# Elementwise work beside two chunked recurrences: POOL to VectorE, a norm by heads on ScalarE, and a later fetch

## The chip, the cores and the metric

The kernel runs on one core of a Trainium2 chip. Five engines work beside each other, each through its own instruction queue in order: PE (TensorE matmul; PEld is its weight load), DVE (VectorE), ACT (ScalarE), POOL (GpSimd) and SP (SyncE, which here only issues DMAs). The metric is the device time of one execution in microseconds (us).

## The reference, cut to what matters

Two residual layers over 2048 tokens of width 1024 and a final norm. Layer 0 mixes by retention (4 heads) and stick-breaking attention (4 heads); layer 1 is an RWKV-7 recurrence with 16 heads of 64. After each layer an embedding `p[i]` is projected, gated and added.

```python
def block(args):                                   # stick-breaking, per block of 128 queries
    z = jnp.einsum('bqhd,bkhd->bhqk', q_blk, k) * scale
    log_1mb = jnp.where(mask, log_sigmoid(-z), 0.0)
    after = lax.cumsum(log_1mb, axis=3, reverse=True) - log_1mb
    w = jnp.where(mask, jnp.exp(log_sigmoid(z) + after), 0.0)
    return jnp.einsum('bhqk,bkhd->bqhd', w, v)

def step(state, inp):                              # RWKV-7, per token
    sk = jnp.einsum('bhvk,bhk->bhv', state, kk_t)
    state = state*w_t - sk*(kk_t*a_t) + v_t*k_t
    return state, jnp.einsum('bhvk,bhk->bhv', state, r_t)

y = head_norm(y, LNX_EPS) * lnx_g + lnx_b          # mean and variance over the 64 of a head
y = y + sum(r*k*r_k) * v                           # "bonus"
h = h + (y*silu(g)) @ w_out
h = h + sigmoid(h @ ple_gate) * (p @ ple_proj)
```

## The kernel before, in words

All large products are split into three fp32r products (high and low parts of both factors, `mm3`, L258 to L260), each 128 by 128 by 512; below they are called dense products. The sequence is done in two halves of 1024 tokens. The stages in order of time: layer 0's mixers of the first half, its tail (`tail`) and layer 1's projections (`l1_proj`); layer 0's mixers of the second half (to about 1900 us, the stick-breaking attention last); then the first half's recurrence merged with layer 0's tail of the second half; `l1_proj` of the second half; the second half's recurrence merged with layer 1's tail of the first half and of the first 512 tokens of the second; and a last tail block of 512 tokens.

The attention (L682 to L721) scores two blocks of 128 queries against up to 512 keys: PE computes z, ACT two sigmoids, DVE a reversed running product `rr` (the scan, L712), POOL copies the carry (L711) and multiplies `be` by `rr` (L721), PE transposes `be`, ACT and DVE split the result (L218, L219) and PE multiplies by the values.

A recurrence (`recur`) has 16 chunks of 64 tokens. Each chunk has small 64-wide products: `gram` (L1490, for the chunk three ahead; none for the last three), `inv` (a triangular inverse, one chunk ahead), and the state chain `chunk`: x (L1615), u (L1593), s (L1630), y. The next state is formed at L1638 and L1639 on two halves of the partitions, `par` 0 on DVE and `par` 1 on POOL. `post` norms the y of the chunk before: mean on DVE, subtraction on POOL (L1670), square on ACT (L1671), variance on DVE, scaling, `lnx` gain and bonus on POOL (L1675, L1677, L1678).

The merged tails (`tail_lean`) work on blocks of 512 tokens: eight output columns of the out projection, then eight of the gate projection (24 dense products each), the latter with 6 of the embedding's (`pp`). `gated` fetches the next block's inputs (L943 and on: DMA `stage` and `g`, two multiplications on DVE, a sigmoid), one column ahead of each gate column. The third block of the last merged stage reads what the recurrence beside it has just written, and is `may` only when its first eight chunks are done (`self.ready`).

`merge` hands out the two streams' instructions by fixed costs (`COST`, `RATIO`), the recurrence with a lead in priority. A scheduler then orders every engine's queue by a modelled timeline; so an operation that changes engine also moves others.

Of the kernel before, what the change touches and what calls it, by code (L numbers as in the profile page):

```python
# [9 lines left out]
F32 = mybir.dt.float32  # L10
# [3 lines left out]
AF = mybir.ActivationFunctionType  # L14
ALU = mybir.AluOpType
# [6 lines left out]
NB = D // P  # L22
# [8 lines left out]
C = 64  # L31
# [102 lines left out]
class Trunk:  # L134
# [520 lines left out]
    def attention(self, w, es):  # L655

        nc, tc, dd = self.nc, self.tc, self.dd
# [9 lines left out]
        def attn(h):  # L667
# [3 lines left out]
            for g in (0, 1) if w == 0 else (2, 1, 0, 3):  # L671
# [3 lines left out]
                vt = sb.tile([P, 2, 4, P], F32R, tag="vg", name=self.u("vg"), bufs=4)  # L675
# [6 lines left out]
            def unit(qp, g, st):  # L682
                i0 = w * NTT + qp * 2
                carry = st["carry"]
                kt, vt = kv[g]
# [7 lines left out]
                for qi in range(2):  # L693
# [14 lines left out]
                    if carry[qi] is None:  # L708
                        nc.gpsimd.memset(rr[:, kw : kw + 1], 1.0)
                    else:  # L710
                        nc.gpsimd.tensor_copy(rr[:, kw : kw + 1], carry[qi])  # L711
                    nc.vector.tensor_tensor_scan(  # L712
# [7 lines left out]
                    carry[qi] = rr[:, 0:1]  # L720
                    nc.gpsimd.tensor_tensor(be, be, rr[:, 1 : kw + 1], op=ALU.mult)  # L721
                    c = be
# [195 lines left out]
    def tail_lean(self, es, parts):  # L918


        nc, i = self.nc, self.i
# [42 lines left out]
        def block(blk, staged, following):  # L964
# [39 lines left out]
            for ob in range(NB):  # L1004
# [10 lines left out]
                nwt = self.w_cols(i["ple_gate"][l], (ob + 1) * P, f"gate{l}") if ob + 1 < NB else None  # L1015
                if following:
                    while not following[0][-1]():
                        yield 1.0
                    ahead.append(gated(following, ob))
                yield from proj(wt, hs)  # L1020
# [8 lines left out]
                o = T("o", 2)  # L1029
                nc.gpsimd.tensor_tensor(o, hs[ob][0].bitcast(F32), hs[ob][1].bitcast(F32), op=ALU.add)  # L1030
                nc.vector.tensor_tensor(o, o, g, op=ALU.add)
                yield 1.3
                if ob == 0:
                    nc.scalar.activation(self.ssacc[:, sl], o, AF.Square)
                else:
                    nc.scalar.activation(g, o, AF.Square)
                    nc.gpsimd.tensor_tensor(self.ssacc[:, sl], self.ssacc[:, sl], g, op=ALU.add)
                if l == 1:
                    nc.vector.tensor_scalar_mul(o, o, self.col(V_GF, ob))
                nc.sync.dma_start(h1[:, ob, sl], o)  # L1040
                yield
            return ahead

# [384 lines left out]
    def recur(self, w, es, lean=False, early=0):  # L1428
# [178 lines left out]
        def chunk(s):  # L1607
# [27 lines left out]
            for par in range(2):  # L1635
                hs = half(par)
                nx = tmp[hs] if last else st[s + 1]["w"][hs, 0, par]
                nc.vector.tensor_tensor(tmp[hs], ps[hs], sv[hs, par], op=ALU.add)  # L1638
                (nc.gpsimd if par else nc.vector).tensor_tensor(  # L1639
                    nx, tmp[hs], self.pc[hs, :, s].unsqueeze(2).to_broadcast([64, NB, C]), op=ALU.mult  # L1640
                )
# [20 lines left out]
        def post(s):  # L1662
# [5 lines left out]
            nc.vector.tensor_reduce(mean, y, axis=mybir.AxisListType.X, op=ALU.add)  # L1668
            nc.vector.tensor_scalar_mul(mean, mean, 1.0 / C)
            nc.gpsimd.tensor_tensor(y, y, bc(mean), op=ALU.subtract)  # L1670
            nc.scalar.activation(sq, y, AF.Square)  # L1671
            yield
            nc.vector.tensor_reduce(var, sq, axis=mybir.AxisListType.X, op=ALU.add)
            rs = self.rsqrt(fin, var, 1.0 / C, LNX_EPS, NB, "yr")
            nc.gpsimd.tensor_tensor(y, y, bc(rs), op=ALU.mult)  # L1675
            yield
            nc.gpsimd.tensor_tensor(vt, vt, bc(bonus[:, s]), op=ALU.mult)  # L1677
            nc.gpsimd.tensor_tensor(y, y, lnx[0][0], op=ALU.mult)  # L1678
            nc.vector.tensor_tensor(vt, vt, lnx[1][0], op=ALU.add)
            yield  # L1680
# [210 lines left out]
```

## Time and profile before

| | us |
|---|---|
| median of 3 runs | 3787.74 (3785.84 to 3797.48) |
| the profiled execution | 3787.24 |
| its span, first to last instruction | 3785.5 |
| PE busy in the span | 3536.1 (93%) |
| DVE busy | 1954.3 (52%) |
| ACT busy | 1412.1 (37%) |
| POOL busy | 986.2 (26%) |

Busy shares are unions over the whole span. PE's small products overlap, so the sum over its groups is more than its busy time. The granted TensorE clock is a share of full speed: 1.00 is 2.4 GHz, 0.50 is 1.2 GHz, and what lies between is a mix of the two within a stretch.

### The profile page before, as it was taken

How to read it: one execution, taken by the hardware profiler on the slowest of the kernel's cores; microseconds unless marked ns; L12 is line 12 of the kernel's file. 1: busy time of each engine (PE TensorE's matmuls, PEld its weight loads, DVE VectorE, ACT ScalarE, POOL GpSimd, SP SyncE). 2: the span in 40 equal slices, each digit the busy share in tenths (PEclk: the TensorE clock that was granted, in tenths of full speed). 3: DMA queues.
4: the chain of work that ended last, by engine and by line, in shares of the span. 5: the costliest groups of instructions: out<-in, count | busy, mean ns of one | idle time of the engine just before them, and what ended most of it. 6: DMA issues, size and time to landing. Idle time of an engine off the chain costs nothing.

```text
span 3785.5 us, 66193 instructions
## 1 busy us (share of the span) xinstructions
PE 3536.1 (93%) x25929; PEld 2801.1 (74%) x25929; DVE 1954.3 (52%) x3884; ACT 1412.1 (37%) x2767; POOL 986.2 (26%) x1036
## 2 busy tenths in 40 slices
PE   8999999899999999998979999899988799999978
PEld 6888877777666788887767777677656677777757
DVE  4334541453675433457956756542574477567532
ACT  5233453344553221445522322243553233223233
POOL 4345543400000222455512312200000143122322
PEclk9999999999999999999969999599989799989989
DMA  6348866655587225546456665343575876556485
GB/s 234 103 170 268 226 191 208 208 168 177 194 260 272 74 95 171 174 107 134 88 150 203 177 179 150 110 143 123 185 240 179 203 226 200 156 166 197 161 284 179
DMA packets 593792, 675.14 MB, mean 178 GB/s; under 512 B 215764, under 2 KB 443976, under 8 KB 562504
## 3 DMA queue, kind: packets, MB, share of 16 engines
q1 hardware_dynamic: 510056, 577.95, 49.3%
q10 hardware_dynamic: 42848, 59.39, 4.4%
q0 software_dynamic: 40576, 33.56, 4.2%
q8 instruction: 205, 3.36, 0.4%
q14 instruction: 107, 0.88, 0.1%
HBM read 414.78 MB, written 255.98 MB: 177 GB/s over the span
## 4 chain that ended last, share of the span: by engine, by line
PE 32%; DMA 8%; DVE 7%; SPq 3%; ACT 1%; issue 1%; POOL 1%; ACTq 0%; POOLq 0%; DVEq 0%
PE pj L258 6%; PE pj L259 6%; PE pj L260 6%; PE g L1490 2%; PE y L1652 2%; PE s L1630 1%; PE y L1649 1%; DMA wraw<-in_odd_w_out 1%; DMA w<-parts 1%; PE u L1593 1%; DMA g<-g 1%; DVE prd L1521 1%; PE x L1615 1%; PE kt L1603 1%; DVE wb L1527 1%
## 5 line engine op out<-in xcount | busy, mean ns | idle before, releaser
L258 PE MATMUL pj<-act,w 128*128 128x512 f32 x1216 | 498.5, 414 | 20.3 <-ACT act L218 9.8
L260 PE MATMUL pj<-act,w 128*128 128x512 f32 x1216 | 498.2, 410 | 4.0 <-POOL w L219 4.0
L259 PE MATMUL pj<-act,w 128*128 128x512 f32 x1216 | 496.6, 409 | 0.4 <-POOL act L219 0.4
L258 PE MATMUL pj<-xs,w 128*128 128x512 f32 x768 | 298.4, 403 | 18.1 <-DMA w<-parts 6.5
L259 PE MATMUL pj<-xs,w 128*128 128x512 f32 x768 | 307.0, 400 | 5.2 <-DVE xs L219 5.1
L260 PE MATMUL pj<-xs,w 128*128 128x512 f32 x768 | 302.4, 397 | 0.0
L258 PEld LDWEIGHTS pj<-act,w 128*128 128x128 f32 x1216 | 237.8, 196 | 72.0 <-ACT act L218 11.3
L260 PEld LDWEIGHTS pj<-act,w 128*128 128x128 f32 x1216 | 237.7, 195 | 56.4 <-POOL w L219 4.9
L259 PEld LDWEIGHTS pj<-act,w 128*128 128x128 f32 x1216 | 238.5, 196 | 50.5 <-POOL act L219 0.8
L258 PE MATMUL pj<-w,act 128*128 128x512 f32 x640 | 259.0, 408 | 10.8 <-ACT sg L535 7.1
L712 DVE TENSOR_TENSOR_SCAN rr<-om,rr,ones 128x512 f32<-128x512 f32 (+3 forms) x160 | 216.7, 1361 | 77.1 <-ACT om L706 68.6
L259 PE MATMUL pj<-w,act 128*128 128x512 f32 x640 | 254.9, 398 | 0.0
L260 PE MATMUL pj<-w,act 128*128 128x512 f32 x640 | 253.5, 399 | 0.0
L721 POOL TENSOR_TENSOR be<-be,rr 128x512 f32<-128x512 f32 (+3 forms) x160 | 167.3, 1048 | 192.6 <-DVE rr L712 87.2
L219 POOL TENSOR_TENSOR w<-wraw,w 128x1024 fp32r<-128x1024 f32 x72 | 159.4, 2218 | 173.4 <-ACT w L218 152.1
L258 PEld LDWEIGHTS pj<-xs,w 128*128 128x128 f32 x768 | 146.9, 192 | 67.2 <-issue 15.6
L1490 PE MATMUL g<-xr,kb 64*128 64x128 f32 x1024 | 149.7, 309 | 34.9 <-DVE grb L1498 20.6
L259 PEld LDWEIGHTS pj<-xs,w 128*128 128x128 f32 x768 | 146.9, 191 | 43.5 <-DVE xs L219 11.8
L260 PEld LDWEIGHTS pj<-xs,w 128*128 128x128 f32 x768 | 147.0, 192 | 34.3 <-issue 3.3
L1490 PEld LDWEIGHTS g<-xr,kb 64*128 64x128 f32 x1024 | 121.6, 203 | 60.0 <-DVE grb L1498 22.2
L258 PEld LDWEIGHTS pj<-w,act 128*128 128x128 f32 x640 | 121.9, 191 | 39.2 <-ACT sg L535 10.3
L218 ACT CAST w<-wraw 128x1024 fp32r<-128x1024 f32 x105 | 104.4, 1000 | 123.0 <-PE pj L260 27.2
(364 smaller groups left out, 7760.2 us busy)
## 6 DMA issues: line engine op xcount, KB each, us to landing
w<-parts SPq DMA_DIRECT2D x145, 1024.0 KB
parts<-w SPq DMA_DIRECT2D x97, 1024.0 KB
wraw<-in_odd_w_in SPq DMA_DIRECT2D x32, 512.0 KB
ar<-ar SPq DMA_DIRECT2D x32, 512.0 KB
w<-v SPq DMA_DIRECT2D x128, 128.0 KB
xr<-ar SPq DMA_DIRECT2D x64, 256.0 KB
kb<-kb SPq DMA_DIRECT2D x32, 512.0 KB
kg<-dk POOLq DMA_DIRECT2D x24, 512.0 KB, 5.0
```

The source lines that it names most:

```text
L218: nc.scalar.copy(hi, src)
L219: (lo_eng or nc.vector).tensor_tensor(lo, src, hi.bitcast(F32), op=ALU.subtract)
L258: nc.tensor.matmul(ps, a[0], b[0], start=first, stop=False)
L259: nc.tensor.matmul(ps, a[0], b[1], start=False, stop=False)
L260: nc.tensor.matmul(ps, a[1], b[0], start=False, stop=last)
L712: nc.vector.tensor_tensor_scan(rr[:, 0:kw][:, ::-1], om[:, ::-1], self.ones.to_broadcast([P, kw]), rr[:, kw : kw + 1], op0=ALU.mult, op1=A ...
L721: nc.gpsimd.tensor_tensor(be, be, rr[:, 1 : kw + 1], op=ALU.mult)
L1490: nc.tensor.matmul(ps[:, j], kb[br, 4 * g + j], xr[br, par, 4 * g + j], start=True, stop=True)
L1521: nc.vector.tensor_tensor(pr[:, :k, :n], nb[:, m, k:].unsqueeze(1).to_broadcast([P, k, n]), wb[:, :k, m:k].to_broadcast([P, k, n]), op=ALU ...
L1527: nc.vector.tensor_tensor(wb[:, :k, k:], wb[:, :k, k:], pr[:, :k, :n], op=ALU.add)
L1593: nc.tensor.matmul(ps[hs, ob], lhs[hs, ob], rhs[hs, ob], start=True, stop=True)
L1652: nc.tensor.matmul(o, d["grb"][hs, ob], uv[hs, par, ob], start=False, stop=True)
```

## The change

On the engines: the attention's carry copy and product, the recurrence's second half of the next state, the bonus and gain products of the norm, and the tail's two additions go from POOL to VectorE. The norm of a chunk is done by heads on ScalarE: eight squares with the mean as bias and a sum taken along (which replace subtraction, square and variance), and eight scalings. The carried-out `gated` of a following block is taken up at a column only if the block may be read; if not, all that is missing is fetched at the end. What stays on POOL beside the recurrences is the split of weights that are read for the first time (L219) and DMAs.

```diff
@@ attention
-                        nc.gpsimd.tensor_copy(rr[:, kw : kw + 1], carry[qi])
+                        nc.vector.tensor_copy(rr[:, kw : kw + 1], carry[qi])
...
-                    nc.gpsimd.tensor_tensor(be, be, rr[:, 1 : kw + 1], op=ALU.mult)
+                    nc.vector.tensor_tensor(be, be, rr[:, 1 : kw + 1], op=ALU.mult)
@@ tail_lean
-                if following:
-                    while not following[0][-1]():
-                        yield 1.0
-                    ahead.append(gated(following, ob))
+                if following and following[0][-1]():
+                    ahead.append(gated(following, len(ahead)))
...
-                nc.gpsimd.tensor_tensor(o, hs[ob][0].bitcast(F32), hs[ob][1].bitcast(F32), op=ALU.add)
+                nc.vector.tensor_tensor(o, hs[ob][0].bitcast(F32), hs[ob][1].bitcast(F32), op=ALU.add)
...
-                    nc.gpsimd.tensor_tensor(self.ssacc[:, sl], self.ssacc[:, sl], g, op=ALU.add)
+                    nc.vector.tensor_tensor(self.ssacc[:, sl], self.ssacc[:, sl], g, op=ALU.add)
...
+            while following and len(ahead) < NB:
+                while not following[0][-1]():
+                    yield 1.0
+                ahead.append(gated(following, len(ahead)))
@@ recur, chunk
-                (nc.gpsimd if par else nc.vector).tensor_tensor(
+                nc.vector.tensor_tensor(
@@ recur, post
-            nc.vector.tensor_scalar_mul(mean, mean, 1.0 / C)
-            nc.gpsimd.tensor_tensor(y, y, bc(mean), op=ALU.subtract)
-            nc.scalar.activation(sq, y, AF.Square)
-            yield
-            nc.vector.tensor_reduce(var, sq, axis=mybir.AxisListType.X, op=ALU.add)
+            nc.vector.tensor_scalar_mul(mean, mean, -1.0 / C)
+            for o in range(NB):
+                nc.scalar.activation(
+                    sq[:, o], y[:, o], AF.Square, bias=mean[:, o : o + 1], accum_out=var[:, o : o + 1]
+                )
+            nc.vector.tensor_tensor(vt, vt, bc(bonus[:, s]), op=ALU.mult)
+            yield
             rs = self.rsqrt(fin, var, 1.0 / C, LNX_EPS, NB, "yr")
-            nc.gpsimd.tensor_tensor(y, y, bc(rs), op=ALU.mult)
-            yield
-            nc.gpsimd.tensor_tensor(vt, vt, bc(bonus[:, s]), op=ALU.mult)
-            nc.gpsimd.tensor_tensor(y, y, lnx[0][0], op=ALU.mult)
+            nc.vector.tensor_tensor(mean, mean, rs, op=ALU.mult)
+            for o in range(NB):
+                nc.scalar.activation(
+                    y[:, o], y[:, o], AF.Identity, scale=rs[:, o : o + 1], bias=mean[:, o : o + 1]
+                )
             nc.vector.tensor_tensor(vt, vt, lnx[1][0], op=ALU.add)
+            yield
+            nc.vector.tensor_tensor(y, y, lnx[0][0], op=ALU.mult)
```

Three places in the order. First VectorE near the end of the second half's attention (`rr` the scan, `wT` the split weights, `xr` and `grb` the recurrence's gram, `tds` its inverse, `wb` and `prd` the inner inverse). Before:

```order
L712 SCALAR_TENSOR_TENSOR rr_16094<-om_16093,rr_16094,ones 128x384
L1494 TENSOR_TENSOR xr_17604<-g_17842,k 64x512
L1576 COPY f_3410_17449<-f_3409_17432 32x256
L1498 TENSOR_TENSOR grb_17840<-g_17842,k 64x256
L219 TENSOR_TENSOR wT_16058<-tp_16066,wT_16057 128x4x128
L712 SCALAR_TENSOR_TENSOR rr_16107<-om_16106,rr_16107,ones 128x512
L219 TENSOR_TENSOR wT_16114<-tp_16115,wT_16113 128x4x128
L712 SCALAR_TENSOR_TENSOR rr_16150<-om_16149,rr_16150,ones 128x512
```

The same place now:

```order
L721 TENSOR_TENSOR be_16160<-be_16160,rr_16162 128x512
L712 SCALAR_TENSOR_TENSOR rr_16201<-om_16200,rr_16201,ones 128x512
L711 COPY rr_16213<-rr_16162 128x1
L1523 TENSOR_TENSOR prd_17455<-nb_17417,wb_17418 128x3x13
L219 TENSOR_TENSOR wT_16169<-tp_16170,wT_16168 128x3x128
L1544 STREAM_TRANSPOSE t_3337_16917<-tds_16371 128x512
L721 TENSOR_TENSOR be_16199<-be_16199,rr_16201 128x512
L712 SCALAR_TENSOR_TENSOR rr_16213<-om_16212,rr_16213,ones 128x512
```

Each scan now has its product and copy in the same queue, and the recurrence stands further back: from the first gram to the last scan there are four pairs of `xr` and `grb` and 23 rows of `prd` and `wb` fewer than before, and the first chunk's u and s products follow the attention's last, where before 35 z products came behind its first s products.

Second, PE where the tail's dense products end beside the first recurrence (`pp` the embedding's, `t` and `f` the inverse, `ssp` the sums of squares, which are the tail's last). Before, at the fourteenth chunk's u:

```order
L258 MATMUL pp_20696<-pT_18543,pw_20611 128x512
L259 MATMUL pp_20696<-pT_18544,pw_20611 128x512
L260 MATMUL pp_20696<-pT_18543,pw_20611 128x512
L1583 MATMUL t_4022_22416<-tds_16371,f_4018_22384 32x32 x16
L1081 MATMUL ssp_23337<-ones,ssacc 128x1 x4
L1593 MATMUL u_22545<-xs_22522,tds_16371 64x64
L1686 MATMUL yt_22482<-k,y_21993 128x128 x4
```

Now the same end stands at the twelfth chunk's u:

```order
L259 MATMUL pp_20787<-pT_18570,pw_20702 128x512
L1585 MATMUL t_3946_21874<-tds_16372,f_3942_21844 32x32 x16
L260 MATMUL pp_20787<-pT_18569,pw_20702 128x512
L1492 MATMUL g_22208<-xr_21963,kb_21966 128x128 x4
L1595 MATMUL u_22008<-xs_21985,tds_16372 64x64
L1492 MATMUL g_22253<-xr_21963,kb_21966 128x128 x4
L1083 MATMUL ssp_23545<-ones,ssacc 128x1 x4
```

From the second chunk to there the tail's 864 dense products stand in ten chunks, where they stood in twelve; four chunks follow that have none, where two did.

Third, SP's queue where the last merged stage fetches the third block (`stage` from the recurrence's output `yT`, `g` its gate). Before:

```order
L946 DMA stage_32424<-yT_26660 128x512
L946 DMA stage_32597<-yT_26660 128x512
L1464 DMA kb_31774<-kb_23272 128x8x128
L949 DMA g_31709<-g_23277 128x512
L1040 DMA h_4714_26658<-o_31651 128x512
```

Now:

```order
L946 DMA stage_32056<-yT_26868 128x512
L1466 DMA kb_32548<-kb_23480 128x8x128
L946 DMA stage_32063<-yT_26868 128x512
L949 DMA g_32030<-g_23485 128x512
L949 DMA g_32037<-g_23486 128x512
```

The gates' fetches followed one by one between the second block's stores; now the second block is over first. On PE the interval from the ninth to the tenth chunk of this recurrence has no dense product (18 before), that from the fifteenth to the sixteenth has 2 (78 before), and none is left behind the sixteenth (24 before).

## Rows read from the trace of the kernel before

**Rows 1.** The page's first part: busy time, share and instructions of each engine.

```profile
PE 3536.1 (93%) x25929; PEld 2801.1 (74%) x25929; DVE 1954.3 (52%) x3884; ACT 1412.1 (37%) x2767; POOL 986.2 (26%) x1036
```

**Rows 2.** Busy time in stretches: stretch, length, engines with counts, PEclk, DMA share, GB/s.

```profile
1740.00:1900.00 160.00, 143.59 (x1374) 121.05 (x1373) 143.74 (x222) 93.33 (x205) 87.83 (x124) 0.96 0.43 91
1900.00:1990.00 90.00, 70.35 (x878) 55.71 (x878) 47.79 (x116) 21.01 (x43) 13.25 (x11) 0.70 0.59 168
1990.00:2380.00 390.00, 381.80 (x4820) 299.63 (x4819) 246.76 (x578) 115.44 (x237) 99.36 (x80) 0.97 0.62 179
2380.00:2400.00 20.00, 20.00 (x237) 16.38 (x237) 11.59 (x47) 4.16 (x8) 6.80 (x6) 0.53 0.27 83
3020.00:3500.00 480.00, 461.20 (x5674) 358.67 (x5674) 318.39 (x734) 154.42 (x306) 139.71 (x104) 0.93 0.66 190
```

**Rows 3.** Groups by line, attention's end, 1720 to 1905; the last from 1740.

```profile
L712 DVE TENSOR_TENSOR_SCAN rr<-om,rr,ones 128x512 f32<-128x512 f32 (+3 forms) x57 | 74.2, 1302 | 0.9 <-ACT om L706 0.3
L219 DVE TENSOR_TENSOR wT<-tp,wT 128x512 fp32r<-128x512 f32 (+3 forms) x61 | 38.1, 630 | 14.3 <-ACT wT L218 13.4
L1494 DVE TENSOR_TENSOR xr<-g,k 64x512 f32<-64x512 f32 x20 | 13.7, 683 | 12.0 <-PE g L1490 11.8
L1521 DVE TENSOR_TENSOR prd<-nb,wb 128x39 f32<-128x39 f32 (+7 forms) x26 | 9.5, 364 | 0.4
...
L711 POOL COPY rr<-rr 128x1 f32<-128x1 f32 x40 | 16.1, 401 | 10.4 <-DVE prd L1521 5.1 <-DVE rr L712 5.1
...
L712 DVE TENSOR_TENSOR_SCAN rr<-om,rr,ones 128x512 f32<-128x512 f32 x44 | 62.5, 1421 | 0.8 <-ACT om L706 0.3
```

**Rows 4.** Groups by line, whole span: VectorE with and without POOL beside it.

```profile
L1370 DVE TENSOR_TENSOR_SCAN L<-scan,sg 128x512 f32<-128x512 f32 x32 | 39.2, 1224 | 88.0 <-ACT sg L1363 88.0
L219 DVE TENSOR_TENSOR act<-stage,act 128x512 fp32r<-128x512 f32 x80 | 66.1, 846 | 13.1 <-ACT act L218 9.6 <-PE pj L259 1.5 <-PE pj L260 1.3
L219 DVE TENSOR_TENSOR xs<-mxa,xs 128x512 fp32r<-128x512 f32 x128 | 88.6, 702 | 96.0 <-ACT xs L218 95.1
L1639 DVE TENSOR_TENSOR w<-xs,pc 64x512 f32<-64x512 f32 x30 | 30.4, 1015 | 0.3
```

**Rows 5.** Instructions of single lines: count, ns minimum/median/maximum, first and last start, form.

```profile
L1669 DVE TENSOR_SCALAR mean<-mean x32: 153/172/1256, 1908.4 to 3622.0; 128x8 f32<-128x8 f32 x32
L384 ACT ACTIVATION_READ_ACCUMULATOR sq<-x x8: 186/186/187, 5.9 to 19.4; 128x1 f32 x8
L1563 ACT COPY tds<-t x64: 238/257/259, 1834.7 to 3583.7; 16x128 f32<-16x128 f32 x64
L1671 ACT ACTIVATE t<-y x30: 617/622/635, 1909.9 to 3604.8; 128x512 f32<-128x512 f32 x30
```

**Rows 6.** PE in order of time: u of chunks 2, 4, 14, 15, 16; the tail's first dense product.

```profile
1911.01 1.97 PE L1593 MATMUL u<-xs,tds 64*64 64x64 f32 x32 [1.34 <-ACT xs L1617]
...
1932.21 0.79 PE L258 MATMUL pj<-act,w 128*128 128x512 f32 x1
...
2003.75 1.15 PE L1593 MATMUL u<-xs,tds 64*64 64x64 f32 x32
...
2376.30 0.33 PE L1593 MATMUL u<-xs,tds 64*64 64x64 f32 x2
...
2411.19 0.47 PE L1593 MATMUL u<-xs,tds 64*64 64x64 f32 x2 [0.46 <-ACT tds L1586]
...
2439.66 0.47 PE L1593 MATMUL u<-xs,tds 64*64 64x64 f32 x2 [0.46 <-ACT tds L1586]
```

**Rows 7.** VectorE in order of time: the attention's last scan.

```profile
1895.42 1.27 DVE L712 TENSOR_TENSOR_SCAN rr<-om,rr,ones 128x512 f32<-128x512 f32 x1
```

**Rows 8.** PE in order of time: two dense products that follow each other.

```profile
2469.81 0.39 PE L260 MATMUL pj<-xs,w 128*128 128x512 f32 x1
2470.04 0.39 PE L259 MATMUL pj<-xs,w 128*128 128x512 f32 x1
```

More of the change, by code (lines that the diff above doesn't have):

```diff
@@ L1668, in post @@
             nc.vector.tensor_reduce(mean, y, axis=mybir.AxisListType.X, op=ALU.add)
-            nc.vector.tensor_scalar_mul(mean, mean, 1.0 / C)
-            nc.gpsimd.tensor_tensor(y, y, bc(mean), op=ALU.subtract)
-            nc.scalar.activation(sq, y, AF.Square)
+            nc.vector.tensor_scalar_mul(mean, mean, -1.0 / C)
[4 more added lines that the diff above has]
+            nc.vector.tensor_tensor(vt, vt, bc(bonus[:, s]), op=ALU.mult)
             yield
-            nc.vector.tensor_reduce(var, sq, axis=mybir.AxisListType.X, op=ALU.add)
             rs = self.rsqrt(fin, var, 1.0 / C, LNX_EPS, NB, "yr")
-            nc.gpsimd.tensor_tensor(y, y, bc(rs), op=ALU.mult)
+            nc.vector.tensor_tensor(mean, mean, rs, op=ALU.mult)
[3 more added lines that the diff above has]
+                )
+            nc.vector.tensor_tensor(vt, vt, lnx[1][0], op=ALU.add)
             yield
-            nc.gpsimd.tensor_tensor(vt, vt, bc(bonus[:, s]), op=ALU.mult)
-            nc.gpsimd.tensor_tensor(y, y, lnx[0][0], op=ALU.mult)
-            nc.vector.tensor_tensor(vt, vt, lnx[1][0], op=ALU.add)
+            nc.vector.tensor_tensor(y, y, lnx[0][0], op=ALU.mult)
             yield
```

## The prediction, made before the kernel ran

> **What bounds the kernel now.** I read the busy line first: PE works 93% of the span, no other engine more than 52% [rows 1]. The reader is to see that work taken from POOL or given to VectorE counts only where PE waits for it. So I went to the stretches that the change touches, by windows [rows 2]. Beside the first recurrence, 1990 to 2380, PE is busy 381.80 of 390.00 us at a clock of 0.97; beside the second, 3020 to 3500, 461.20 of 480.00 at 0.93: PE is the bound in both, with VectorE at 63% and 66% and ScalarE near 30%. Two stretches differ. At the attention's end, 1740 to 1900, VectorE (143.74 of 160) is as full as PE (143.59). From 2380 to 2400, where the tail's dense products have run out, PE counts as busy for all 20.00 us, but at a clock of 0.53, near the lower level of 1.2 GHz: it works through one recurrence's chain of small products. Next I read groups by line at the attention's end [rows 3] and over the whole span [rows 4], single lines for prices [rows 5], and PE in order of time, for when each chunk's u product comes [rows 6]. What the change does to PE's order stands in the orders shown above; these u times price it.
>
> **Unit prices.** A dense product takes 0.23 us, from one start to the next [rows 8]. From the u of chunk 4 to that of chunk 14 are 372.55 us [rows 6]; 721 of the tail's dense products stand there in PE's order, 165.8 us, so an ordinary chunk costs (372.55 − 165.8) / 10 = 20.7 us without them. Chunks 2 to 4 take 92.74 us with the other 143 of the 864 (32.9), thus 29.9 each: a start loss of 9.2 a chunk, 18.4 in all. The two chunks without dense products take 34.88 and 28.47 [rows 6], mean 31.7, which is 11.0 above an ordinary chunk's own cost. That a dense-free chunk costs 11.0 more is the number on which most hangs.
>
> **Attention's end.** VectorE gets a product beside each of 57 scans and 40 copies. The nearest row for the product is L219's wT at 0.630 [rows 3], 35.9 us; for the copy a small VectorE operation of 0.172 [rows 5], 6.8 us (between nothing and POOL's own 16.1 [rows 3]). It is relieved in two ways. The scans took 1.421 us with POOL at work, the same operation in L1370 1.224 without [rows 3, 4]: 44 × 0.197 = 8.7. And four pairs of gram operations at 0.683 and 23 inner products at 0.364 [rows 3] now stand behind the last scan: 13.9. Left are 42.7 − 8.7 − 13.9 = 20.1 us more, against 16.3 us of VectorE idle [rows 2]. If all of that idle time can be used, the last scan comes 3.8 later, if none, 20.1. VectorE is the full engine and gets more than it gives away, so a gain is excluded; but PE's 16.4 idle us there leave room for no delay at all. Ends 0 and 21; I take +6, near the end at which the idle time is used.
>
> **The first chunk.** Now u and s of chunk 1 follow the attention's last products. Before, u of chunk 2 came at 1911.01, 14.3 us after the last scan's end at 1896.69 [rows 6, 7]. With 10 us from that scan to u of chunk 1 (an estimate, part of those 14.3) and a dense-free chunk of 28.47 to chunk 2, it would come 38.5 after: +24. But the tail's first dense product came only at 1932.21 [rows 6], 35.5 us after the scan, and from 1900 to 1990 PE was busy for just 70.35 of 90 at a clock of 0.70 [rows 2]: the first chunk can lie in that hole, and the end would then be 0. I take +10, between ends 0 and 24.
>
> **Chunks 2 to 16 of the first recurrence.** The same 864 products stand in ten chunks, and four have none. New: 864 × 0.23 + 10 × 20.7 + 4 × 31.7 = 532.5; before: 92.74 + 372.55 + 34.88 + 28.47 = 528.6. That is +4, with the start loss gone. If it stays, +22. On the other side the ordinary chunks could lose what PE idles (8.2 us of 390) and what the clock takes (0.03 of 381.8, 11.5 us), 18.8 over the ten chunks: −15. I take +4.
>
> **The second recurrence.** The interval from chunk 9 to 10 loses its last 18 dense products, that from 15 to 16 all but 2 of 78, and the 24 behind chunk 16 go; they fill other chunks, so the products themselves cancel. The two empty intervals cost 11.0 each: +22, and that is the upper end. From 3020 to 3500 there is more to win than in the first: 18.8 us idle, and 0.04 × 480 = 19 if the clock rises from 0.93 to 0.97 [rows 2], together 38. All of it would give −16; half of it about +2, which I take. On SP the fetches only come later; what is queued behind the block's waiting fetches there are stores and gram inputs three chunks ahead, which I put at nothing.
>
> **What ScalarE and VectorE get beside the recurrences.** Eight squares of 128 by 64 lie between a 16 by 128 copy (0.257) and the 128 by 512 operation (0.622) [rows 5]; near the small end, at 0.33, and with 0.186 for reading each sum they take 4.1 us. Eight scalings take 2.6, and the old square's 0.62 goes: 6.1 us more a chunk. With 10.5 chunks in 390 us ScalarE goes from 30% to about 46%. In an ordinary chunk PE's dense products cover this; without that cover up to 4.1 us of squares stand ahead of the state's copies. VectorE gets some six operations a chunk of 0.7 to 1.0 us, and sheds a reduction. The second half of the next state no longer runs beside the first on POOL but behind it; in return L1639 should fall from 1.015 towards the 0.702 of an undisturbed operation [rows 4], so the chain grows by about 0.702 − 0.313 = 0.4 us a chunk. At 66% VectorE covers that in ordinary chunks; seven empty chunks would pay 3 us. I cost the two edits at nothing here and keep both prices for the third rival.
>
> **Sum.** 6 + 10 + 4 + 2 = +22 on the profiled execution's 3787.24, thus 3809; the median of the runs is 0.5 higher, which changes nothing. The lower ends give 0 + 0 − 15 − 16 = −31 (3756), the upper ones 21 + 24 + 22 + 22 = +89 (3876), where every term would have to fall badly at once.
>
> **Rivals.** *Faster: POOL held VectorE.* An instruction whose price falls with POOL gone shows it: L219 on `act` took 0.846 in the mean where the same operation on `xs` took 0.702 [rows 4], 80 × 0.144 = 11.5 us. If PE's waits in ordinary chunks come from such VectorE work, they close, and both delays at the start lie in the hole before the tail: the lower ends, about 3756. Against it: PE idles only 2% beside the first recurrence. It decides if an ordinary chunk falls below about 20.7 − 2 us. Beside this row stands a rule of the Trainium skill ("SBUF — State Buffer", Who interferes with whom): a VectorE instruction with two inputs in SBUF contends with a GpSimd instruction that reads SBUF. By that rule, the trace agrees on `act` and on the scans.
>
> *No change.* The delays of attention and first chunk (16) lie in the dense-free hole up to 1932, and what is gained in fuller chunks pays for the empty ones (+4 and +2): 3793, or 3788 if these vanish too. For it speaks the hole's size of 35.5 us, against it that VectorE is full there.
>
> *Slower by much: ScalarE's squares in the empty chunks.* Seven chunks then have no cover: 1 to 2, 12 to 16 in the first recurrence, and 9 to 10 and 15 to 16 in the second. If the 4.1 us stand ahead of the copies that the state waits for, 7 × 4.1 = 29 come on top: 3838. The engine's 30% speaks against it.
>
> *The empty chunks stay at full clock.* The 11.0 us more of a dense-free chunk would then go, and six such chunks (four and two) give 66 back: 3743. The row from 2380 to 2400 is against it, with PE busy for 20.00 of 20.00 at 0.53 [rows 2]. The Trainium skill ("TensorE: Matmul & The Clock Gate", What's actually happening) says that the clock follows how busy PE has been of late; by that rule, a PE that counts as wholly busy should have the upper level, and the trace does not bear it out for small products in a chain.
>
> **How the numbers follow.** The forecast, with its own range of 3792 to 3830 (the first two terms nearly hidden, or both near their upper ends), gets 0.41. Faster through POOL's absence 0.25, no change 0.20, ScalarE 0.11, full clock 0.03. About 0.3% is what a measurement of this kernel can tell from no change, so faster is below 3776, slower above 3799. The forecast puts 0.05 into no change; of the faster case 0.01 falls there, of the no-change case 0.01 on either side. Faster: 0.24 + 0.03 + 0.01 = 0.28; same: 0.18 + 0.05 + 0.01 = 0.24; slower: 0.36 + 0.11 + 0.01 = 0.48. The range from 3748 to 3846 leaves out the full clock, the outer part of the faster case and of ScalarE's.
>
> **What will show it.** The last scan's end near 1903 instead of 1896.69 and u of chunk 2 near 1927 bear out the first two terms; the last scan no later than 1897 refutes the first. From the u of chunk 12 to that of 16 some 127 us at a clock near 0.5 bear out the empty chunks; under 100 refutes them. An ordinary chunk (u to u, less 0.23 for each dense product) at 20 to 21 us bears out the third term, at 18 it makes the first rival true. L219 on `act` and L1639 both near 0.70 show that VectorE is free of POOL; if PE's idle time stays at 2% and 4% all the same, that freedom was worth nothing. In the second recurrence the intervals 9 to 10 and 15 to 16 should be near 30 us. ScalarE's squares ahead of a copy that PE waits for, seen in PE's waits of the empty chunks, would show the third rival. I am wrong in sign if the ordinary chunks gain more than the empty ones cost.

## The result and the profile after

The changed kernel takes 3825.31 us in the median (3816.67 to 3826.32, 4 runs) against 3791.24; the ratio is 1.0106, 95% interval 1.0081 to 1.0130. Its profiled execution, 3816.67 us, is the shortest of the four; its span is 3814.4 us, 28.9 more than before. All stage times below are from that execution, so they account for 28.9 us of a loss that is 34 us by the two medians and 40 by the ratio.

The page's first line of the changed kernel (before: [rows 1]):

```profile
PE 3538.2 (93%) x25929; PEld 2811.6 (74%) x25929; DVE 2017.9 (53%) x4311; ACT 1565.0 (41%) x3503; POOL 485.5 (13%) x545
```

PE's busy time is the same within about 2 us. What is longer is its idle time: 3814.4 − 3538.2 = 276.2 us against 3785.5 − 3536.1 = 249.4. The windows of the changed kernel, columns as in [rows 2]:

```profile
1740.00:1900.00 160.00, 139.61 (x1289) 117.08 (x1288) 142.58 (x284) 85.35 (x184) 13.45 (x29) 0.91 0.32 68
1900.00:1990.00 90.00, 79.64 (x970) 63.68 (x970) 50.95 (x133) 33.00 (x95) 0.00 (x0) 0.85 0.73 210
1990.00:2380.00 390.00, 371.03 (x4608) 294.90 (x4608) 246.73 (x644) 159.75 (x455) 0.00 (x0) 0.91 0.62 178
2380.00:2400.00 20.00, 13.08 (x187) 10.54 (x186) 12.80 (x38) 7.58 (x20) 0.00 (x0) 0.57 0.44 107
3020.00:3500.00 480.00, 452.88 (x5535) 355.86 (x5531) 306.83 (x760) 202.74 (x548) 33.15 (x18) 0.89 0.67 191
```

Beside the recurrences POOL is empty or nearly so, VectorE is no busier than before, ScalarE has some 45 us more, and PE's busy time and clock are both lower (0.97 to 0.91, 0.93 to 0.89). With all the edits together, the relief of POOL did not shorten these stretches. For the stages, PE in order of time: u of chunks 2, 12 to 16 of the first recurrence with the tail's first dense product, and of chunks 1, 9, 10 and 16 of the second.

```profile
1911.03 0.47 PE L1595 MATMUL u<-xs,tds 64*64 64x64 f32 x2 [0.95 <-ACT tds L1588]
1923.65 0.80 PE L258 MATMUL pj<-act,w 128*128 128x512 f32 x1
2320.65 0.27 PE L1595 MATMUL u<-xs,tds 64*64 64x64 f32 x1
2364.30 0.37 PE L1595 MATMUL u<-xs,tds 64*64 64x64 f32 x1 [0.46 <-ACT tds L1588]
2393.52 0.37 PE L1595 MATMUL u<-xs,tds 64*64 64x64 f32 x1 [0.46 <-ACT tds L1588]
2421.27 0.37 PE L1595 MATMUL u<-xs,tds 64*64 64x64 f32 x1 [0.46 <-ACT tds L1588]
2446.53 0.37 PE L1595 MATMUL u<-xs,tds 64*64 64x64 f32 x1 [0.46 <-ACT tds L1588]
3031.14 0.27 PE L1595 MATMUL u<-xs,tds 64*64 64x64 f32 x1
3373.29 0.37 PE L1595 MATMUL u<-xs,tds 64*64 64x64 f32 x1 [0.46 <-ACT tds L1588]
3403.09 0.36 PE L1595 MATMUL u<-xs,tds 64*64 64x64 f32 x1
3630.76 0.37 PE L1595 MATMUL u<-xs,tds 64*64 64x64 f32 x1 [0.46 <-ACT tds L1588]
```

The kernel before has u of the second recurrence's chunks 1 and 16 at:

```profile
3018.54 0.27 PE L1593 MATMUL u<-xs,tds 64*64 64x64 f32 x1
...
3600.43 0.27 PE L1593 MATMUL u<-xs,tds 64*64 64x64 f32 x1
```

The attention's last scan of the changed kernel (before: [rows 7]):

```profile
1872.82 1.27 DVE L712 TENSOR_TENSOR_SCAN rr<-om,rr,ones 128x512 f32<-128x512 f32 x1
```

| stage, us | before | after | difference | predicted |
|---|---|---|---|---|
| to the last scan's end | 1896.69 | 1874.09 | −22.6 | +6 |
| from there to u of chunk 2 | 14.3 | 36.9 | +22.6 | +10 |
| u of chunk 2 to 16 | 528.7 | 535.5 | +6.8 | +4 |
| to u of the second recurrence's chunk 1 | 578.9 | 584.6 | +5.7 | 0 |
| its u of chunk 1 to 16 | 581.9 | 599.6 | +17.7 | +2 |
| to the end of the span | 185.1 | 183.6 | −1.4 | 0 |

The stage of the second recurrence does not hold the same work in both kernels: the dense products between its u of chunk 1 and u of chunk 16 are 1125 before and 1168 now, and those behind it 475 and 432, as counted in the traces. The 43 that moved are 9.9 us of work at 0.23 us each, and the stage that they left is only 1.4 us shorter.

### The profile page after: what moved, and what is told of

Read it like the earlier page. It is cut to its first block, busy times and chain, and to the rows that moved or that the text cites. A ratio compares the mean times of both kernels' runs of the same rounds, so it can differ in the third digit from the quotient of the medians.

```text
span 3814.4 us, 66378 instructions
## 1 busy us (share of the span) xinstructions
PE 3538.2 (93%) x25929; PEld 2811.6 (74%) x25929; DVE 2017.9 (53%) x4311; ACT 1565.0 (41%) x3503; POOL 485.5 (13%) x545
## 5 line engine op out<-in xcount | busy, mean ns | idle before, releaser
L258 PE MATMUL pj<-act,w 128*128 128x512 f32 x1216 | 495.5, 412 | 26.2 <-DVE r L799 9.0
L258 PEld LDWEIGHTS pj<-act,w 128*128 128x128 f32 x1216 | 234.9, 194 | 78.6 <-DVE r L799 9.9
L260 PEld LDWEIGHTS pj<-act,w 128*128 128x128 f32 x1216 | 235.2, 193 | 54.3 <-POOL w L219 4.5
L259 PEld LDWEIGHTS pj<-act,w 128*128 128x128 f32 x1216 | 235.8, 194 | 51.2 <-DVE act L219 2.3
L712 DVE TENSOR_TENSOR_SCAN rr<-om,rr,ones 128x512 f32<-128x512 f32 (+3 forms) x160 | 195.9, 1228 | 54.0 <-ACT om L706 53.1
L219 POOL TENSOR_TENSOR w<-wraw,w 128x1024 fp32r<-128x1024 f32 x72 | 160.8, 2238 | 290.5 <-ACT w L218 252.8
```

Source lines behind the costliest of these rows:

```text
L219: (lo_eng or nc.vector).tensor_tensor(lo, src, hi.bitcast(F32), op=ALU.subtract)
L258: nc.tensor.matmul(ps, a[0], b[0], start=first, stop=False)
L259: nc.tensor.matmul(ps, a[0], b[1], start=False, stop=False)
L260: nc.tensor.matmul(ps, a[1], b[0], start=False, stop=last)
L712: nc.vector.tensor_tensor_scan(rr[:, 0:kw][:, ::-1], om[:, ::-1], self.ones.to_broadcast([P, kw]), rr[:, kw : kw + 1], op0=ALU.mult, op1=A ...
```

## The experiments

Twelve kernels ran, each over five rounds beside the kernel before; they are named by what they start from (a: the changed kernel, b: the kernel before). "Edits" in the table are attention (A), fetch (F), next state and tail additions (S), norm (N). Idle is the span less PE's busy time, clock the mean granted one, both of the one profiled execution. These single executions lie up to 18 us from their kernel's median, so only what holds for whole groups is read from them.

| kernel | edits | ratio to before, 95% | PE idle, us | clock |
|---|---|---|---|---|
| before | | 1 | 249 | 0.943 |
| changed | A F S N | 1.0106 [1.0081, 1.0130] | 276 | 0.933 |
| a_old_norm | A F S | 0.9937 [0.9914, 0.9961] | 257 | 0.949 |
| a_norm_vector | A F S, old norm all on VectorE | 1.0031 [1.0011, 1.0050] | 256 | 0.939 |
| a_heads_pool | A F S N, two products on POOL | 1.0101 [1.0079, 1.0122] | 283 | 0.936 |
| a_heads_squares | A F S, half of N | 1.0098 [1.0080, 1.0117] | 292 | 0.933 |
| a_idle_squares | A F S, idle narrow operations | 1.0112 [1.0094, 1.0129] | 280 | 0.930 |
| a_ratio_b | A F S N, other merge constant | 1.0111 [1.0084, 1.0138] | 285 | 0.934 |
| a_fill192 | A F S N, 192 more products | 1.0128 [1.0107, 1.0149] | 281 | 0.943 |
| b_only_heads | N | 1.0083 [1.0065, 1.0102] | 279 | 0.936 |
| b_only_fetch | F | 1.0000 [0.9977, 1.0023] | 269 | 0.943 |
| b_attn_fetch | A F | 1.0023 [1.0007, 1.0039] | 264 | 0.940 |
| b_state_adds | S | 1.0037 [1.0018, 1.0057] | 255 | 0.943 |
| b_state_adds_fetch | S F | 1.0045 [1.0031, 1.0060] | 260 | 0.941 |

**Which part costs.** The first theory was the prediction's: time goes where the order leaves chunks without dense products. The fetch alone:

```diff
-                if following:
-                    while not following[0][-1]():
-                        yield 1.0
-                    ahead.append(gated(following, ob))
+                if following and following[0][-1]():
+                    ahead.append(gated(following, len(ahead)))
...
```

> The kernel before with one edit of the change alone: the third block's inputs fetched when ready, those missing at the block's end. Theory 1 (the time goes where the order has recurrence chunks without dense products): the first recurrence is ordered as before (two empty chunks at its end, 528.7 us from u of chunk 2 to u of chunk 16), in the second no chunk is empty and 20 products move from behind chunk 16 between the chunks; total within 0.3% of before, if anything 0 to 5 us shorter (ratio 0.998 to 1.002). Rival (the later fetch itself delays the third block): second recurrence some 15 us longer, ratio 1.004.

Measured 1.0000 [0.9977, 1.0023]: neither a gain nor a cost that can be told. The norm put back as it was (`post` with POOL's subtract and products, one wide square):

```diff
-            for o in range(NB):
-                nc.scalar.activation(sq[:, o], y[:, o], AF.Square, bias=..., accum_out=...)
+            nc.gpsimd.tensor_tensor(y, y, bc(mean), op=ALU.subtract)
+            nc.scalar.activation(sq, y, AF.Square)
...
```

> The changed kernel with the old norm (subtraction, gain, bonus and scaling on POOL, one wide square on ScalarE); all other edits stay. Its order has three empty chunks at the end of the first recurrence (after: four, before: two) and none in the second (after: one, and one with two products). Theory 1 (empty chunks): u2 to u16 of the first about 532 us (before 528.7, after 535.5), u1 to u16 of the second within 5 us of before's 581.9; ratio to before about 1.002. Rival (VectorE's added work in attention and tail costs the time): at least three quarters of the loss stay, ratio 1.008 or more. By the rival of ScalarE's squares in front of the state's copies the ratio falls to 1.002 too; it is told apart by the empty chunks, which would then be 4 us shorter each than the 25 to 29 us of after.

Measured 0.9937, better than either kernel and than every theory said. Its three empty chunks (31.2, 34.5 and 23.7 us) are no shorter than the last three of the changed kernel (29.2, 27.8 and 25.3, after a first of 43.7), so it is not there that the squares cost, as the third rival had it. Most of the gain lies in the two recurrences: 517.9 and 575.0 us against 535.5 and 599.6. In the first, one empty chunk fewer goes with it, which at the prediction's 11.0 us would be some 11 of the 17.6; in the second, where the dense products of the stage are nearly as many (1173 and 1168), 24.6 us are gained.

**Are empty chunks the cause?** The constant of the second merge:

```diff
-RATIO_B = 0.95
+RATIO_B = 1.02
```

> The changed kernel with one constant of the merge changed (RATIO_B 0.95 to 1.02): the same instructions, the first recurrence ordered alike, in the second no chunk without dense products (the fewest 20, 26 and 32, against 0 and 2). Theory 1 (empty chunks): u1 to u16 of the second falls from 599.6 to 582 to 588 us, total 12 to 18 us below after (ratio to before about 1.006). Rival (the new instructions on VectorE and ScalarE make every chunk of the second dearer): it stays at 595 to 600, ratio 1.010.

Measured 1.0111, and 607.5 us from u of chunk 1 to 16 of the second recurrence. Filling the empty intervals there gained nothing, where the theory promised 12 to 18 us: for the second recurrence it falls. In the first, eight more columns of the gate projection whose results are not used:

```diff
+                lw = wt
...
+            if l == 0 and not following:
+                for _ in range(8):
+                    yield from proj(lw, hs)
+                    done.pop()
```

> The changed kernel with 192 dense products more behind the first merged tail, whose results are not used: beside the recurrence they fill two of the four empty chunks. At 0.23 us they are 44.2 us of work. Theory 1 with the predicted price (an empty chunk costs 11 us more than an ordinary one beyond its products): u2 to u16 of the first recurrence goes from 535.5 to about 558, total +22 on after (ratio to before about 1.0165). If an empty chunk costs no more than any other (the clock and the idle time are not the loss): 580, total +44 (1.022). If the empty chunks hide the products wholly: 536, total as after.

The u of chunks 2 and 16 in this run:

```profile
1910.98 0.37 PE L1600 MATMUL u<-xs,tds 64*64 64x64 f32 x1 [0.89 <-ACT tds L1593]
...
2472.67 0.37 PE L1600 MATMUL u<-xs,tds 64*64 64x64 f32 x1 [0.46 <-ACT tds L1593]
```

That is 561.7 us, 26.2 more than in the changed kernel, for 44.2 us of products: two empty chunks gave back 18.0, thus 9.0 each (priced at 11.0). That is a reading of two single executions. The whole kernel is only 8 us longer than the changed one by the ratios (1.0128 for 1.0106) and 13 by the medians, where the theory had 22 (1.0165). So an empty chunk of the first recurrence has a price, 9.0 us by this reading; but PE still idles 281 us in the whole kernel, and the loss stays.

**What of the norm costs.** Two kernels split the norm. All of it wide, on VectorE (against a_old_norm; the same for scaling, bonus and gain):

```diff
-            nc.gpsimd.tensor_tensor(y, y, bc(mean), op=ALU.subtract)
+            nc.vector.tensor_tensor(y, y, bc(mean), op=ALU.subtract)
...
```

> The changed kernel with the old wide norm, but subtraction, scaling, bonus and gain on VectorE instead of POOL; the square is one wide ScalarE operation. POOL stays as empty as in the changed kernel; nothing is done by heads. The run with the old norm on POOL came to 0.9937 of before, so the norm is where the change loses. Theory 1 (the sixteen narrow ScalarE operations of a chunk, and the order that they lead to, cost the time): as with the old norm, ratio 0.992 to 0.998. Rival (VectorE gets too much when POOL has nothing): as the changed kernel, ratio 1.008 to 1.013.

Or by heads on ScalarE, with two products on POOL (against the changed kernel):

```diff
-            nc.vector.tensor_tensor(vt, vt, bc(bonus[:, s]), op=ALU.mult)
+            nc.gpsimd.tensor_tensor(vt, vt, bc(bonus[:, s]), op=ALU.mult)
...
-            nc.vector.tensor_tensor(y, y, lnx[0][0], op=ALU.mult)
+            nc.gpsimd.tensor_tensor(y, y, lnx[0][0], op=ALU.mult)
```

> The changed kernel with the norm by heads on ScalarE, but bonus and gain products on POOL. Theory 1 (narrow ScalarE operations): ratio 1.008 to 1.013, like the changed kernel. Rival (VectorE's load): ratio at or below 1.000.

Measured 1.0031 and 1.0101. By heads on ScalarE costs 1.0101 − 0.9937 = 1.6% even when POOL helps; the norm all on VectorE costs 1.0031 − 0.9937 = 0.9%. a_heads_pool came as theory 1 said. a_norm_vector met neither expectation: it lies between the two, so work on VectorE has a price too. The norm's edit alone, on the kernel before (the whole `post` part of the change and no other line):

> The kernel before with the norm's edit alone (by heads on ScalarE, bonus and gain on VectorE). Theory 1 (the narrow ScalarE operations and the order that they lead to): slower by 30 to 60 us, ratio 1.008 to 1.016; the time at the lower clock in both recurrences rises from 198 us by 50 or more. Rival (the norm costs only together with VectorE's other new work): ratio 0.998 to 1.004.

Measured 1.0083, with 538.2 and 607.6 us in the recurrences. In the two together TensorE's clock stood at its lower level for 251 us, against 198 before, as theory 1 said. Then the dose, with only the eight squares by heads:

```diff
-            for o in range(NB):
-                nc.scalar.activation(y[:, o], y[:, o], AF.Identity, scale=..., bias=...)
+            nc.vector.tensor_tensor(y, y, bc(rs), op=ALU.mult)
+            nc.vector.tensor_tensor(y, y, bc(mean), op=ALU.add)
```

> The changed kernel with the squares by heads on ScalarE, but the scaling as two wide VectorE operations: eight narrow operations a chunk (about 4.2 us with their sums) in place of sixteen (7.6). Without any, all on VectorE, the ratio was 1.0031, with sixteen 1.0106. Theory 2 (ScalarE's time): in between, 1.005 to 1.008. Rival (the order's chunks without dense products decide: four in the first recurrence as in the changed kernel, none in the second): 1.003 to 1.005.

Measured 1.0098, more than either theory said: with half the narrow operations the loss is nearly whole. This is no clean dose, though: the other half was replaced by two wide operations on VectorE, whose work has a price of its own, as the norm on VectorE showed. And the narrow operations without their use, added to the best kernel:

```diff
+            dum = TF("dum", [P, NB], 1)
+            for o in range(NB):
+                nc.scalar.activation(sq[:, o], y[:, o], AF.Square, accum_out=dum[:, o : o + 1])
             nc.scalar.activation(sq, y, AF.Square)
...
+            for o in range(NB):
+                nc.scalar.activation(sq[:, o], y[:, o], AF.Square)
             nc.gpsimd.tensor_tensor(y, y, bc(rs), op=ALU.mult)
```

> The changed kernel with the old norm on POOL (which ran at 0.9937 of before), and sixteen squares by heads a chunk added on ScalarE whose results nobody uses: eight with sums in front of the wide square, eight in front of the scaling. Theory 2 (it is ScalarE's time in front of the state's copies, and the order that goes with it, whatever the operations are for): the loss comes back, ratio 1.007 to 1.012, and the copy of x on ScalarE starts about 1.0 us after its last product (0.60 with the old norm, 1.05 in the changed kernel). Rival (the norm's own chain through ScalarE comes too late): 0.992 to 0.997.

Measured 1.0112 against 0.9937 without them: the whole loss, though nobody uses what they compute. The added operations do stand in the norm's own way too, eight of them ahead of its wide square. But that rival has little for it: from the mean's sum to the transposes a chunk's norm takes 37.7 us in the mean against 32.5 in the first recurrence, and 34.4 against 34.3 in the second, which is longer too (593.1 us for 575.0); and POOL's scaling never waited for the second eight, it began 0.17 us or less after `yr` was ready in every chunk. The other part of theory 2 was not borne out: the copy of x started 0.70 us after its last product in the mean, not 1.0, which is hardly later than the 0.60 of a_old_norm.

**What gains beside it.** The next state and the additions on VectorE, without and with the fetch; and the attention's edit with the fetch (each on the kernel before):

```diff
-                (nc.gpsimd if par else nc.vector).tensor_tensor(
+                nc.vector.tensor_tensor(
...
-                nc.gpsimd.tensor_tensor(o, hs[ob][0].bitcast(F32), hs[ob][1].bitcast(F32), op=ALU.add)
+                nc.vector.tensor_tensor(o, hs[ob][0].bitcast(F32), hs[ob][1].bitcast(F32), op=ALU.add)
...
```

> The kernel before with two edits alone: the next state's second half and the tail's two additions on VectorE. The old norm with all other edits ran at 0.9937, the attention's edit with the later fetch at 1.0023. Theory (these two are what gains): ratio 0.990 to 0.996, shorter in both recurrences. Rival (they gain only with the others, or the prediction's nothing holds): 0.998 to 1.002. The order has one empty interval in the second recurrence (chunk 9 to 10).

> The same two edits with the later fetch, which fills the empty interval from chunk 9 to 10 of the second recurrence; the first recurrence is ordered alike. If an empty chunk costs 9 to 11 us there, as the run with 192 more products showed for the first recurrence, the ratio is 0.002 to 0.003 below that of the two edits alone; if the later fetch is worth nothing, as when it was done alone, the two are the same.

> The kernel before with the attention's copy and product on VectorE and the later fetch; norm, next state and tail additions as before. The prediction gave the attention's part and the first chunk +16 us; the trace of the changed kernel shows u of chunk 2 at 1911.03 as before (1911.01). Theory 1 (the gain that the old norm showed comes from the attention's edit and its order): ratio 0.993 to 0.997. Rival (it comes from next state and additions on VectorE): ratio 0.998 to 1.003. By the prediction's first two terms: 1.004.

Measured 1.0037, 1.0045 and 1.0023. Both theories of the gain fall: neither part gains by itself, and together they make 0.9937. The fetch filled the empty interval from chunk 9 to 10 (47 dense products where there were none) and gave nothing again. The effects of the edits don't add up; each edit also gives a new order.

## Why the prediction came out as it did

The sign was right, and the median lies 16 us above the forecast (3825 for 3809), inside its range. The size is in good part luck. By stages, the first two terms were to give +16 and gave nothing, while the second recurrence and what lies around it gave +22 (17.7 + 5.7 − 1.4) where +2 was forecast. By edits, the norm, which was put at nothing, costs 1.0106 − 0.9937 = 1.7%, some 64 us, and the other edits together save 0.6%, some 24 us, which the forecast did not have: two errors of opposite sign. The rival that gave ScalarE's squares a price (3838) named the right engine and the wrong place.

**Attention's end: sign wrong.** The groups of the changed kernel from 1720 to 1905, against [rows 3]:

```profile
L712 DVE TENSOR_TENSOR_SCAN rr<-om,rr,ones 128x512 f32<-128x512 f32 (+3 forms) x54 | 63.7, 1181 | 0.9 <-ACT om L706 0.6
L219 DVE TENSOR_TENSOR wT<-tp,wT 128x512 fp32r<-128x512 f32 (+3 forms) x58 | 36.2, 625 | 3.7 <-ACT wT L218 3.2
L721 DVE TENSOR_TENSOR be<-be,rr 128x512 f32<-128x512 f32 (+3 forms) x55 | 34.5, 627 | 0.2
...
L711 DVE COPY rr<-rr 128x1 f32<-128x1 f32 x39 | 5.3, 137 | 0.0
```

The prices held (product 0.627 for 0.630, copy 0.137 for 0.172, and the scans' mean over all shapes fell from 1.302 to 1.181). VectorE from 1720 to the end of the last scan, before and now, columns as in [rows 2]:

```profile
1720.00:1896.69 176.69, 154.71 (x1454) 131.17 (x1454) 147.75 (x228) 99.81 (x220) 100.27 (x144) 0.96 0.52 109
```
```profile
1720.00:1874.09 154.09, 132.81 (x950) 111.52 (x949) 143.87 (x270) 87.77 (x189) 17.35 (x36) 0.92 0.47 96
```

The prediction's sum had 20.1 us more work for VectorE and 16.3 us of idle time to put it in. In fact VectorE is busy 143.87 us against 147.75, so its work did not grow: cheaper scans, three scans fewer in this stretch and recurrence work that stands behind it pay for products and copies. And its idle time fell from 28.9 us to 10.2, which is 18.7 of the 22.6 gained. Ahead of `wT` it waited 13.4 us for ScalarE before and 3.2 now. So the step that failed is "gets more than it gives away, so a gain is excluded". By the scans: from 1720 one came every (1896.69 − 1720) / 57 = 3.10 us before and every (1874.09 − 1720) / 54 = 2.85 now, and the attention stood three scans further on at 1720, which the sum did not reckon with.

**The first chunk.** The step said 38.5 us from the scan to u of chunk 2, and took only +10 of its +24 since part would be hidden. It is 36.9, near the whole. As it began from an earlier scan, the two terms cancel; u of chunk 2 stands at 1911.03 where it was 1911.01. No run shows why they cancel so exactly.

**The first recurrence.** 535.5 us against 532.5 by the sum: the four empty chunks took 125.9 (126.8 by the sum, though in unequal parts, 43.7, 29.2, 27.8 and 25.3), the ten others 409.6 − 198.7 = 210.9 (207). The sum held within 3 us, but one reading in it was off. The prediction's counts of dense products, and those given with the order, run from the s product of a chunk to that of another, its times from u to u. From the u of chunk 4 to that of chunk 14 there are 743 in the trace, not 721, so an ordinary chunk cost 20.2 us before and not 20.7, and the sum would be 527. In that light the ordinary chunks became dearer by 0.9 us each (21.1), where the prediction has the products cover the new work.

**The second recurrence** was mis-sized: +17.7 instead of +2, inside its end of +22. Two steps failed. "The products themselves cancel" did not hold for the stage: the 43 dense products that stood behind the u of chunk 16 (24 by the count from s) add 9.9 us of work to it, and hardly anything is won behind it. And "half of 38" did not come: from 3020 to 3500 the clock fell from 0.93 to 0.89 instead of rising, and PE idles 27.1 us instead of 18.8. The empty intervals were there (9 to 10: 29.8 us; 15 to 16: 23.0 where some 30 were forecast), but an order without them, in a_ratio_b, won nothing.

**The norm at nothing** was wrong, and it is the largest miss. The groups of the whole span after:

```profile
L1681 ACT ACTIVATE y<-y,mean,yr 128x64 f32<-128x64 f32 x256 | 89.2, 428 | 45.4 <-DVE mean L1679 45.1
...
L1673 ACT ACTIVATE t<-y,mean 128x64 f32<-128x64 f32 x240 | 79.9, 335 | 4.4 <-DVE mean L1671 4.2
L219 DVE TENSOR_TENSOR act<-stage,act 128x512 fp32r<-128x512 f32 x80 | 55.9, 719 | 7.2 <-ACT act L218 6.4 <-PE pj L259 0.4
L1673 ACT ACTIVATION_READ_ACCUMULATOR t<-y,mean 128x1 f32 x240 | 45.2, 188 | 0.0
L1641 DVE TENSOR_TENSOR w<-xs,pc 64x512 f32<-64x512 f32 x60 | 43.1, 718 | 1.2
L1676 DVE TENSOR_TENSOR vt<-vt,bon 128x512 f32<-128x512 f32 x32 | 22.1, 691 | 57.5 <-DMA vt<-v 57.5
```

One by one the squares were priced well (0.335 + 0.188 for 0.33 + 0.186), and a scaling takes 0.428 for 0.33; but they overlap, so ScalarE's busy time grew by only (1565.0 − 1412.1) / 32 = 4.8 us a chunk, where 6.1 was said. VectorE is as free of POOL as was said: L219 on `act` takes 0.719 for 0.846, L1641 0.718 for 1.015 [rows 4]. This agrees with the rule of the Trainium skill ("SBUF — State Buffer", Who interferes with whom) that a VectorE instruction with two SBUF inputs contends with a GpSimd instruction that reads SBUF.

The step that failed is "In an ordinary chunk PE's dense products cover this", with the norm's two edits costed at nothing: the runs with and without narrow operations show some 64 us. How the operations cost that much is less clear. ScalarE does come later: it also stands still, 45.1 us ahead of the scalings for the mean, and what is queued behind waits along. One case, ScalarE of the changed kernel in order of time:

```profile
3307.18 0.26 ACT L1565 COPY tds<-t 16x128 f32<-16x128 f32 x1 [5.70 <-PE t L1560]
3310.09 1.43 ACT L1681 ACTIVATE y<-y,mean,yr 128x64 f32<-128x64 f32 x4 [2.65 <-DVE mean L1679]
3311.55 0.26 ACT L1565 COPY tds<-t 16x128 f32<-16x128 f32 x1
3311.83 1.43 ACT L1681 ACTIVATE y<-y,mean,yr 128x64 f32<-128x64 f32 x4
3313.29 0.58 ACT L1619 COPY xs<-x 128x512 f32<-128x512 f32 x1
```

and on PE the product whose result that last copy takes, PE's only wait until the copy is done, and the first product that reads the copy:

```profile
3306.91 1.15 PE L1617 MATMUL x<-w,xr 128*64 128x64 f32 x30
...
3310.57 1.13 PE L1492 MATMUL g<-xr,kb 64*128 64x128 f32 x8 [0.67 <-DMA xr<-ar]
...
3324.47 0.33 PE L1595 MATMUL u<-xs,tds 64*64 64x64 f32 x2
```

x is done at 3308.06, its copy starts at 3313.29: 5.2 us behind a wait for the mean and eight scalings. But PE has dense products and gram meanwhile, and the u that reads the copy comes only 10.6 us after it is done: here the products do cover the delay. Of the 153 state copies (`xs`, `w`, `kbt`) from 1900 to 3700, such narrow operations delay 36 in the changed kernel and 19 in a_idle_squares, as counted in the traces. How late ScalarE is on the whole, the wait ahead of its copy of `kt` tells: the idle time that PE's `kt` ended, from 1900 to 3640, in before, a_old_norm, the changed kernel and a_idle_squares. The less ScalarE waits for PE there, the later it is.

```profile
  PE kt L1603: 86.8, 37
```
```profile
  PE kt L1605: 91.4, 40
```
```profile
  PE kt L1605: 54.7, 31
```
```profile
  PE kt L1605: 67.0, 31
```

These delays alone do not make the loss. Between last product and copy lie, summed over all these copies, 63 us before, 89 in a_old_norm, 115 in a_idle_squares and 135 in the changed kernel: against a_old_norm 26 and 45 us more, for losses of 66 and 64, and a_old_norm is faster than the kernel before with the larger sum. And in the two recurrences PE's own waits for ScalarE are 12.5 us in a_old_norm, 8.7 in the changed kernel and 13.9 in a_idle_squares: they did not grow.

On VectorE one wait of PE stands behind the bonus product that moved there. A gram product of the changed kernel on PE, then VectorE in the 4.53 us that PE waits:

```profile
2356.14 1.22 PE L1492 MATMUL g<-xr,kb 64*128 64x128 f32 x4 [4.53 <-DVE grb L1500]
```
```profile
2351.89 0.69 DVE L1676 TENSOR_TENSOR vt<-vt,bon 128x512 f32<-128x512 f32 x1 [1.01 <-DMA vt<-v]
...
2355.67 0.41 DVE L1500 TENSOR_TENSOR grb<-g,k 64x256 f32<-64x256 f32 x1
```

The `grb` product that frees the gram's buffer stands behind the bonus product, which waits 1.01 us for its DMA, and behind five further operations. It is no large part of the loss: with bonus and gain on POOL (a_heads_pool) the ratio is 1.0101 for 1.0106.

**Shown, and not shown.** Shown: every kernel with the narrow ScalarE operations is at 1.0083 or above, with 276 us or more of PE idle time and, but for the one with added products, a clock of 0.936 or below; every kernel without is at 1.0045 or below, with 269 us or less and 0.939 or above; and narrow operations that nobody uses make the whole loss. Also shown is where the time goes. From a_old_norm to the changed kernel the span grows by 55.1 us, of which 19.5 are PE's idle time; to a_idle_squares it grows by 78.2 us (67 by the medians), of which 23.6 are idle time. The rest, 35.6 and 54.6 us, is PE busy for longer at a lower clock (0.933 and 0.930 for 0.949). In the two recurrences the clock stands at its lower level for 146 us in a_old_norm, 253 in the changed kernel and 258 in a_idle_squares.

Not told apart: how much of the loss comes from copies that are late, and how much from the order that the scheduler makes when it plans with these operations (four empty chunks where the old norm has three), and whether the lower clock is more than a consequence of either. No kernel kept one order with and without them. Nor did any add the same ScalarE time in wide operations, so it is not shown that narrowness matters and not the time alone. Open too: why the three other edits gain 0.6% only together, and the 5.7 us between the recurrences.

The best kernel is a_old_norm: the attention, fetch, next state and additions as in the change, the norm as before, 0.9937 [0.9914, 0.9961].

## What to carry to other kernels

An engine at 30% is not free room: here some 155 us of added ScalarE work cost 1.7% of the whole, though PE did not wait longer for ScalarE itself. So price what moves to a quiet engine, and try it alone, before putting it at nothing. Splitting a wide operation by heads multiplies fixed costs: one square of 128 by 64 with its sum took 0.335 + 0.188 us, one of 128 by 512 took 0.622. Count products and take times between the same instructions. Where a scheduler orders the queues, single edits don't add up: test the bundle by taking out one part at a time before keeping it.

## What was not expected of the hardware

The scalings, narrow operations that take a scale and a bias from memory, took 0.428 us for 128 by 64 where 0.33 was expected; the squares, with a bias alone, took the 0.335 that was expected, and the unused squares, with neither, 0.24. The old square took 0.622 for eight times the elements [rows 5], so narrowing saves little. And the tail's filler paid for itself in part: with 192 more products the mean clock rose from 0.933 to 0.943, the level of the kernel before.
